# Norms from transposed columns and a transposed inverse in a gated delta rule, a remade normalized input in two feed-forward layers, and an output product in two equal pieces

## The chip, the cores and the metric

The kernel runs on one NeuronCore of a Trainium2 chip. The metric is the device time of one execution in microseconds (us). Five engines work side by side, each on its own queue of instructions: PE (TensorE, the matrix unit; its weight loads are listed apart as PEld), DVE (VectorE), ACT (ScalarE), POOL (GpSimd) and SP (SyncE), which issues the transfers. They wait for each other by semaphores.

## The reference

Two blocks run one behind the other on 512 tokens of width 1024, with 256 context tokens in the first and 16 meta tokens in the second. All in 32 bit:

```python
x   = x   + 0.5*m2  * swiglu(modulate(rmsnorm(x, g1),   m0, m1),  w1_in, w1_out)   # first FFN, 2816 wide
ctx = ctx + 0.5*mc2 * swiglu(modulate(rmsnorm(ctx, g1), mc0, mc1), w1_in, w1_out)
x   = x + m5 * (mix @ w_mix_out)            # attention and a short convolution
x   = x + 0.5*m8 * swiglu(modulate(rmsnorm(x, g2), m6, m7), w2_in, w2_out)          # second FFN
x   = rmsnorm(x, final_norm)
h   = concat(meta, x)                        # 528 tokens
h   = h + hybrid_mixer(rmsnorm(h))           # stick-breaking attention and the gated delta rule
h   = h + swiglu(rmsnorm(h, g3), w3_in, w3_out)                                      # third FFN
```

`modulate(h, shift, scale)` is `h*(1+scale)+shift`, `swiglu` is `(silu(y @ gate) * (y @ up)) @ out`. In the delta rule each of 8 heads has q and k of 128 features, made to unit length per token (`x * rsqrt(sum(x*x) + 1e-6)`), v of 256, and per chunk of tokens a lower triangular matrix `eye + lower`, with `lower` from `k k^T` and a decay, that has to be inverted.

## The kernel before

Activations lie transposed: features on the partitions, tokens in the columns, 8 tiles of 128 features (`self.x[0..7]`). Every large product in 32 bit is made of three fast ones: weights and activations are split into a rounded high part and the rest (`wh`, `wl`, `yh`, `yl`, `hh`, `hl`), and `mm3` (line 204) issues high by high, high by low and low by high for each k of 128 features. A weight tile of 128 by 1024 comes by DMA (`raw`), ACT copies it into `wh` (line 159) and DVE subtracts for `wl` (line 148); `run` loads one job ahead or two, from few buffers. `later` and `tick` put other work behind a certain matmul step of a job, and a scheduler that runs when the kernel is built sets the final order on each engine from the order in the code, the pools' buffers and such marks.

`ffn` (line 285) is used three times: kind A with 512 + 256 columns of tokens (x and the context), kinds B and C with 512. It has 22 hidden tiles f in three groups of 8, 7 and 7. For each f a gate job and an up job multiply by the 8 k of `yh`, `yl`; then 8 out jobs multiply the group's hidden tiles (`hh`, `hl`) into the 8 output tiles and `fin` adds them to x. `yh` and `yl` hold x times a gain, without the norm's factor r per token, which is multiplied on behind the product (`scaled`: DVE, from PSUM). In kind B the shift of `modulate` is carried as two more columns of `yh`, `yl`: the product is cut at 256 columns and has a piece of 258 beside it, and the extra column is the bias of the Silu and an addend of up. In kind C there is no shift, and one piece of 512. In the out jobs of kind A each product has a piece of 512 and one of 256.

The delta rule (`delta`, line 1250) goes head by head, with projections for later heads (`mm3` again, over 264 or 512 columns) put between. `prep` (line 1315) makes the decay, the norms of q and k and the triangular matrix `L`; for the norms ACT squares `kt` (528 columns) and `qt` (512), and PE sums over the partitions with nine fp32 matmuls against one column of ones (lines 1342 to 1344). Later in `prep` four transposes of `kt` and one of its 16 meta columns (lines 1397, 1398) give `kd`, `kdm` by ACT. A solve by 32 on DVE gives `XT`, and `inverse` (line 1430) extends it to 64 and 128: with `X` the transpose of `XT`, it makes `t1 = M XT`, subtracts `X t1` from `XT` (line 1450) and `t1 X` from `X` (line 1451), and repeats with the mask `m6` in place of `m5`.

Of the kernel before, what the change touches and what calls it, by code (L numbers as in the profile page):

```python
# [18 lines left out]
P = 128  # L19
D = 1024  # L20
KD = 8
# [99 lines left out]
class K:  # L121
# [163 lines left out]
    def ffn(self, kind, w_in, w_out, groups, pool, fin, bg=None, early=None):  # L285
        A_, n = kind == "A", (768 if kind == "A" else 512)
        r = self.r
        hid = {}
# [13 lines left out]
        def scaled(ps, nm, more=False):  # L302
            t = pool.tile([P, 770], F32, name=nm, tag=nm, bufs=2)
# [15 lines left out]
        parts = [(0, 0, 512, 512)] + ([(514, 512, 256, 513)] if A_ else [])  # L319

# [29 lines left out]
        def out(grp, f, last):  # L350
            def go(ws):
                ps = self.mmtile()
                pieces = lambda k: [(hid[grp[k]][0][:, o:o + w], hid[grp[k]][1][:, o:o + w]) for _, o, w, _ in parts]
# [14 lines left out]
        self.run(jobs, bg, hold=() if early else (3,))  # L368

# [73 lines left out]
    def ffn1(self):  # L443
        tc, nc = self.tc, self.nc
        with ExitStack() as es:
# [384 lines left out]
    def ffn2(self):  # L830
        tc, nc = self.tc, self.nc
        with ExitStack() as es:
# [6 lines left out]
            self.tt(gm, self.vec("final_norm", 0, 8), self.vec("norm_mix_gain_2", 0, 8), ALU.mult)  # L839

# [9 lines left out]
            self.ffn("B", self.d["w2i"], self.d["w2o"], [list(range(0, 8)), list(range(8, 15)), list(range(15, 22))], pool, fin)  # L850
# [399 lines left out]
    def delta(self, es, eg, gl, kdl, beta, g5, bd, first, free, tail, last):  # L1250
# [8 lines left out]
        def bank(tag="d"):  # L1259
            return qd.tile([P, 512], F32, name=tag, tag=tag, bufs=2)  # L1260
# [54 lines left out]
        def prep(h):  # L1315
# [78 lines left out]

            ps, psm = bank(), bank()
            for c in range(4):
                self.T.transpose(ps[:, c * P:(c + 1) * P], ch(kt, c), idn)
            self.T.transpose(psm[:16, :P], kt[:, :16], idn)
            kd, kdm = tile_("kd", 512, 2), tile_("kdm", P, 2)
            for c in range(4):  # L1400
                self.act(kd[:, c * P:(c + 1) * P], ps[:, c * P:(c + 1) * P], AF.Copy, scale=kdl[:, c, h:h + 1])
            self.act(kdm[:16], psm[:16, :P], AF.Copy, scale=kdl[:16, 4, h:h + 1])
# [27 lines left out]
        def inverse(h):  # L1430
# [242 lines left out]
```

## Time and profile before

| | us |
|---|---|
| three timed runs | 2592.44, 2593.01, 2593.96 |
| median | 2593.01 |
| the profiled execution | 2592.23 |
| its span in the trace | 2590.4 |
| PE busy in the span | 2552.5 (99%) |
| DVE busy | 1683.8 (65%) |
| ACT busy | 1098.0 (42%) |

The span goes from the first to the last instruction of one execution that the hardware profiler recorded; the time of the execution is 1.8 us more. Busy times of one engine's instructions can overlap for PE, which is a pipeline: the mean of one matmul is longer than the distance from its start to the next one's start. How fast PE goes is therefore read from starts. An fp32 matmul that is not split by the kernel appears as two records. The granted clock (PEclk) is 1.00 at 2.4 GHz and 0.50 at 1.2 GHz. Of the stages, the first FFN ends shortly before 620 us, the attention and its convolution lie in 620 to 860, the second FFN in 860 to 1232, stick-breaking attention and the projections around it before 1515, the delta rule in 1515 to 2176, the third FFN from 2225 to the end.

### The profile page before, as it was taken

What the parts mean: (1) busy time and instruction counts of PE and PEld (TensorE: products, weight loads), DVE (VectorE), ACT (ScalarE), POOL (GpSimd) and SP (SyncE); (2) the same over time, 40 slices, a digit from 0 to 9 for tenths busy, and PEclk for the clock granted to TensorE, in tenths of its full rate; (3) what the DMA queues carried; (4) which work ended last, traced back from release to release, by engine and by line L of the source; (5) the groups of instructions that cost most, each with busy time, mean ns of one, the idle gap of its engine ahead of it and who ended that gap; (6) DMA issues with size and microseconds to landing.
All of it is one profiled execution on the core that took longest, in us unless ns stands there. A gap on an engine that the chain in (4) does not pass through costs nothing.

```text
span 2590.4 us, 37782 instructions
## 1 busy us (share of the span) xinstructions
PE 2552.5 (99%) x14983; PEld 2207.9 (85%) x14983; DVE 1683.8 (65%) x3442; ACT 1098.0 (42%) x1898; POOL 15.5 (1%) x11
## 2 busy tenths in 40 slices
PE   7999999999999999999999999999999999999999
PEld 4888888888897999999888888888888877788887
DVE  7865664356879644446777776878888767444443
ACT  7221221235677422224677752554454444422221
POOL 2000000000000000000000000000000000000000
PEclk8999999999999999999999999999999999999999
DMA  7433643222111333333311122222222222333332
GB/s 262 147 115 98 186 142 119 65 59 75 59 33 46 111 91 97 90 98 85 105 58 58 58 89 77 72 59 75 70 64 76 73 80 90 98 92 95 97 98 83
DMA packets 85265, 235.83 MB, mean 91 GB/s; under 512 B 19840, under 2 KB 22592, under 8 KB 85088
## 3 DMA queue, kind: packets, MB, share of 16 engines
q1 hardware_dynamic: 85088, 233.42, 29.5%
q8 instruction: 118, 1.93, 0.3%
q14 instruction: 59, 0.48, 0.1%
HBM read 228.07 MB, written 5.31 MB: 90 GB/s over the span
## 4 chain that ended last, share of the span: by engine, by line
PE 91%; DVE 4%; ACT 2%; DMA 1%; issue 1%; SPq 0%; DVEq 0%; ACTq 0%
PE mm L204 71%; PE mX L204 3%; PE mT L204 3%; DVE wl L148 1%; PE pt L720 1%; PE pt L730 1%; PE e L1505 1%; PE e L1515 1%; PE pv L1147 1%; PE sx L704 1%; PE e L1497 1%; PE e L1498 1%; PE z L204 1%; PE ap L401 1%; PE e L1511 0%
## 5 line engine op out<-in xcount | busy, mean ns | idle before, releaser
L159 ACT ACTIVATE wh<-raw 128x1024 fp32r<-128x1024 f32 (+2 forms) x371 | 375.1, 1013 | 951.1 <-PE mm L204 650.4
L204 PE MATMUL mm<-yh,wh 128*128 128x512 f32 (+2 forms) x2416 | 683.4, 331 | 9.7 <-ACT yh L159 4.9
L204 PE MATMUL mm<-yl,wh 128*128 128x512 f32 (+2 forms) x2416 | 687.4, 333 | 0.0
L204 PE MATMUL mm<-yh,wl 128*128 128x512 f32 (+2 forms) x2416 | 681.1, 331 | 0.0
L204 PEld LDWEIGHTS mm<-yh,wh 128*128 128x128 f32 x2416 | 409.4, 190 | 56.6 <-issue 6.2
L148 DVE TENSOR_TENSOR wl<-raw,wh 128x1024 fp32r<-128x1024 f32 (+2 forms) x371 | 431.1, 1164 | 37.4 <-ACT wh L159 27.1
L204 PEld LDWEIGHTS mm<-yl,wh 128*128 128x128 f32 x2416 | 409.0, 190 | 42.3 <-issue 1.7
L204 PEld LDWEIGHTS mm<-yh,wl 128*128 128x128 f32 x2416 | 409.4, 190 | 41.1 <-issue 1.4
L204 PE MATMUL mm<-hh,wl 128*128 128x512 f32 x704 | 228.1, 364 | 0.0
L204 PE MATMUL mm<-hl,wh 128*128 128x512 f32 x704 | 227.3, 363 | 0.8 <-DVE hl L148 0.8
L204 PE MATMUL mm<-hh,wh 128*128 128x512 f32 x704 | 227.8, 364 | 0.2 <-ACT hh L159 0.2
L148 DVE TENSOR_TENSOR tu<-mm,r 128x512 f32<-128x512 f32 (+1 forms) x66 | 51.4, 779 | 193.7 <-PE mm L204 193.6
L148 DVE TENSOR_TENSOR tg<-mm,r 128x512 f32<-128x512 f32 (+1 forms) x84 | 64.3, 765 | 124.3 <-PE mm L204 124.2
L204 PEld LDWEIGHTS mm<-hl,wh 128*128 128x128 f32 x704 | 120.0, 188 | 23.0 <-DVE hl L148 1.0
L204 PEld LDWEIGHTS mm<-hh,wh 128*128 128x128 f32 x704 | 120.3, 188 | 22.4 <-ACT hh L159 0.5
L204 PEld LDWEIGHTS mm<-hh,wl 128*128 128x128 f32 x704 | 120.0, 188 | 21.0
L151 DVE SCALAR_TENSOR_TENSOR aacc<-araw,csil,aacc 128x1024 f32<-128x1024 f32 x70 | 88.2, 1282 | 60.6 <-DMA araw<-wada 60.6
L151 DVE SCALAR_TENSOR_TENSOR x<-mm,g,x 128x512 f32<-128x512 f32 x48 | 35.8, 747 | 113.1 <-PE mm L204 113.1
L204 PE MATMUL mm<-ych,wh 128*128 128x258 f32 (+1 forms) x368 | 104.3, 283 | 0.0
L204 PE MATMUL mm<-ycl,wh 128*128 128x258 f32 (+1 forms) x368 | 104.1, 283 | 0.0
L204 PE MATMUL mm<-ych,wl 128*128 128x258 f32 (+1 forms) x368 | 103.9, 282 | 0.0
L159 ACT ACTIVATE hh<-tu 128x512 fp32r<-128x512 f32 x88 | 48.5, 575 | 125.6 <-DVE tu L151 106.9
(493 smaller groups left out, 4121.6 us busy)
## 6 DMA issues: line engine op xcount, KB each, us to landing
raw<-win SPq DMA_DIRECT2D x88, 512.0 KB
araw<-wada SPq DMA_DIRECT2D x60, 512.0 KB
raw<-w1i SPq DMA_DIRECT2D x44, 512.0 KB
raw<-w2i SPq DMA_DIRECT2D x44, 512.0 KB
raw<-w3i SPq DMA_DIRECT2D x44, 512.0 KB
raw<-wmi SPq DMA_DIRECT2D x18, 512.0 KB
raw<-wbd SPq DMA_DIRECT2D x16, 512.0 KB
raw<-w1o SPq DMA_DIRECT2D x16, 448.0 KB
```

The lines of the kernel that those rows point to most:

```text
L148: return self.V.tensor_tensor(out=out, in0=a, in1=b, op=op)
L151: return self.V.scalar_tensor_tensor(out=out, in0=a, scalar=s, in1=b, op0=op0, op1=op1)
L159: return self.A.activation(out=out, in_=a, func=func, bias=bias, scale=scale, **kw)
L204: last = self.T.matmul(o, lhsT=w[a], rhs=yy[b], start=start and i == 0, stop=stop and i == 2)
L401: self.T.matmul(ps[h][:4], lhsT=self.csr4[:, k, :], rhs=w, start=k == 0 and i == 0, stop=k == KD - 1 and i == 1)
L704: self.T.matmul(sx[:, :512], lhsT=lq, rhs=kk[:, :512], start=i == 0, stop=i == 1)
L720: self.T.transpose(ps[:, (2 * kt + qt) * P:(2 * kt + qt + 1) * P], pr[qt][:, (2 * c + kt) * P:(2 * c + kt + 1) * P], self.cs("ident"))
L730: self.T.matmul(ps[:, :256], lhsT=vs[:, kt, g, :], rhs=pp[kt // 2][i][:, (kt % 2) * 256:(kt % 2 + 1) * 256], start=kt == 0 and i == 0, sto ...
L1147: self.T.matmul(pv[:, c0:], lhsT=a[:m, j], rhs=b, start=j == 4 and i == 0, stop=i == 2, skip_group_check=True)
L1497: self.T.matmul(ps[:, :256], lhsT=ch(kt, c), rhs=S0, start=True, stop=True)
L1498: self.T.matmul(ps[:, 256:], lhsT=ch(qt, c, 0), rhs=S0, start=True, stop=True)
L1505: self.T.matmul(ps[:, :256], lhsT=ch(XT, c, 0), rhs=vi, start=True, stop=True)
```

## The change

There are four parts.

First, the out product of kind A is cut into 384 + 384 columns. They lie in columns 128 to 896 of the PSUM tile, so that each half stays in one bank, and `fin` reads x from 128:640 and the context from 640:896.

Second, kinds B and C make a full y while the first jobs run: `remake` forms for each k `z = x * r * gain (+ shift)` on DVE, splits it into `zh` (ACT) and `zl` (DVE), two k in each of the jobs 2 to 5 (counted from 0). From job 8 on, the gate and up jobs multiply by z (`gate2`, `up2`) in one piece of 512 columns, Silu reads PSUM, and no r, no bias and no extra columns are left there. The small `pad` tiles move the addresses.

Third, `prep` transposes `kt` (4 + 1, formerly further on) and `qt` (4, new) and takes the norms by ACT, Square with a sum along the row, one for each 128 tokens; the copies into `kd` and `kdm` stand between them. The nine matmuls against ones are gone.

Fourth, `inverse` no longer makes `t1 X`; the second step's `X` is the transpose of the new `XT`, by four PE transposes and an ACT copy, and the mask `m6` is applied earlier.

```diff
@@ ffn
         def scaled(ps, nm, more=False):
-            t = pool.tile([P, 770], F32, name=nm, tag=nm, bufs=2)
+            t = pool.tile([P, wide], F32, name=nm, tag=nm, bufs=2)
...
+        halves = [(0, 128, 384), (384, 512, 384)] if A_ else [(0, 0, 512)]
+
+        def gate2(f):
+            def go(ws):
+                ps = self.mmtile()
+                self.gemm([ps[:, :512]], ws, KD, remade[1])
+                t = pool.tile([P, wide], F32, name="tg", tag="tg", bufs=2)
+                self.last_silu = self.act(t[:, :512], ps[:, :512], AF.Silu)
+                gu[f] = t
+            return go
+
+        def up2(f, slot):
+            def go(ws):
+                ps = self.mmtile()
+                self.gemm([ps[:, :512]], ws, KD, remade[1])
+                t = pool.tile([P, wide], F32, name="tu", tag="tu", bufs=2)[:, :512]
...
+                self.tt(t, ps[:, :512], gu.pop(f)[:, :512], ALU.mult)
+                self.split(hh, hl, t)
+                hid[f] = (hh, hl)
+            return go
@@ out
-                self.gemm([ps[:, o:o + w] for _, o, w, _ in parts], ws, len(grp), pieces)
+                self.gemm([ps[:, c:c + w] for _, c, w in halves], ws, len(grp), pieces)
@@
-                jobs.append(([(w_in[f], 1024)], gate(f)))
-                jobs.append(([(w_in[NF + f], 1024)], up(f, i)))
+                new = remade and len(jobs) >= remade[0]
+                jobs.append(([(w_in[f], 1024)], (gate2 if new else gate)(f)))
+                jobs.append(([(w_in[NF + f], 1024)], (up2 if new else up)(f, i)))
@@
+    def remake(self, pool, gain, shift):
+
+        hi = [pool.tile([P, S], F32R, name=f"zh{k}", tag=f"zh{k}") for k in range(KD)]
+        lo = [pool.tile([P, S], F32R, name=f"zl{k}", tag=f"zl{k}") for k in range(KD)]
+
+        def one(k):
+            t = pool.tile([P, S], F32, name="zt", tag="zt", bufs=2)
+            self.tt(t, self.x[k], self.r[:, :S], ALU.mult)
+            if shift is None:
+                self.make_y(k, t, gain(k), hi[k], lo[k])
+            else:
+                self.ts(t, t, gain(k), ALU.mult, shift(k), ALU.add)
+                self.split(hi[k], lo[k], t)
+
+        def step(i):
+            if 0 < i <= KD // 2:
+                for k in (2 * i - 2, 2 * i - 1):
+                    self.later(4 * (k % 2) + 1, lambda k=k: one(k))
+        return step, lambda k: [(hi[k], lo[k])]
@@ ffn1, fin
-                self.stt(self.x[f], ps[:, :512], g2[:, 0, f:f + 1], self.x[f], ALU.mult, ALU.add)
-                self.stt(self.ctx[f], ps[:, 512:768], g2[:, 1, f:f + 1], self.ctx[f], ALU.mult, ALU.add)
+                self.stt(self.x[f], ps[:, 128:640], g2[:, 0, f:f + 1], self.x[f], ALU.mult, ALU.add)
+                self.stt(self.ctx[f], ps[:, 640:896], g2[:, 1, f:f + 1], self.ctx[f], ALU.mult, ALU.add)
@@ ffn2
+            g7 = pool.tile([P, 8], F32, name="g7")
+            self.stt(g7, self.mx[:, 7, :], 1.0, self.vec("norm_ffn2", 0, 8), ALU.add, ALU.mult)
+            pad = pool.tile([P, 24], F32, name="pad")
+            nc.vector.memset(pad[:, :1], 0.0)
+            step, y = self.remake(pool, lambda k: g7[:, k:k + 1], lambda k: self.mx[:, 6, k:k + 1])
...
+                     bg=step, remade=(7, y))
@@ delta, prep
-            u = tile_("cu", T, 2)
-            self.act(u, kt, AF.Square)
-            u2 = tile_("cu", T, 2)
-            self.act(u2[:, :S], qt, AF.Square)
-            ps = bank()
-            one = cs("ones", 1)
-            for c in range(4):
-                self.T.matmul(ps[:, c:c + 1], lhsT=ch(u, c), rhs=one, start=True, stop=True)
-                self.T.matmul(ps[:, 5 + c:6 + c], lhsT=ch(u2, c, 0), rhs=one, start=True, stop=True)
-            self.T.matmul(ps[:16, 4:5], lhsT=u[:, :16], rhs=one, start=True, stop=True)
...
-            self.ts(nk[:, 0:4], ps[:, 0:4], EPS, ALU.add)
-            self.ts(nk[:, 5:9], ps[:, 5:9], EPS, ALU.add)
-            self.ts(nk[:16, 4:5], ps[:16, 4:5], EPS, ALU.add)
...
+            ps, psm = bank(), bank()
+            for c in range(4):
+                self.T.transpose(ps[:, c * P:(c + 1) * P], ch(kt, c), idn)
+            self.T.transpose(psm[:16, :P], kt[:, :16], idn)
+            for c in range(4):
+                self.act(u[:, :P], ps[:, c * P:(c + 1) * P], AF.Square, accum_out=nk[:, c:c + 1])
+                self.act(kd[:, c * P:(c + 1) * P], ps[:, c * P:(c + 1) * P], AF.Copy, scale=kdl[:, c, h:h + 1])
+            self.act(u[:16, :P], psm[:16, :P], AF.Square, accum_out=nk[:16, 4:5])
+            self.act(kdm[:16], psm[:16, :P], AF.Copy, scale=kdl[:16, 4, h:h + 1])
+            ps = bank()
+            for c in range(4):
+                self.T.transpose(ps[:, c * P:(c + 1) * P], ch(qt, c, 0), idn)
+            for c in range(4):
+                self.act(u[:, :P], ps[:, c * P:(c + 1) * P], AF.Square, accum_out=nk[:, 5 + c:6 + c])
+            self.ts(nk, nk, EPS, ALU.add)
@@ delta, inverse
-            ps, ps2 = bank(), bank()
-            for c in range(4):
-                self.T.matmul(c_(ps, c), lhsT=c_(X, c), rhs=c_(t1, c), start=True, stop=True)
-                self.T.matmul(c_(ps2, c), lhsT=c_(t1, c), rhs=c_(X, c), start=True, stop=True)
-            self.tt(XT, XT, ps, ALU.subtract)
-            self.tt(X, X, ps2, ALU.subtract)
-            self.tt(m3(M), m3(L), bc(cs("m6")), ALU.mult)
...
+            self.tt(m3(M), m3(L), bc(cs("m6")), ALU.mult)
+            self.tt(XT, XT, ps, ALU.subtract)
+            yield
             ps, ps2 = bank(), bank()
...
             self.act(t1, ps, AF.Copy)
+            for c in range(4):
+                self.T.transpose(c_(ps2, c), c_(XT, c), idn)
+            self.act(X, ps2, AF.Copy)
@@ ffn3
-            pad = pool.tile([P, 144], F32, name="pad")
+            pad = pool.tile([P, 48], F32, name="pad")
+            nc.vector.memset(pad[:, :1], 0.0)
+            step, y = self.remake(pool, lambda k: self.vec("norm_ffn_gain_2", k), None)
+            pad = pool.tile([P, 32], F32, name="pad2")
...
+                     bg=step, remade=(7, y))
```

What the scheduler makes of it on the engines, at three places. First PE in the delta rule, where a head's norms are made; `cst` is the tile of constants (the ones, or the unit matrix of a transpose), `cu` the squares. Before:

```order
L204 MATMUL mm<-yh_78,wl 128x264 x2
L1342 MATMUL d<-cst,cu 128x1
L1364 MATMUL d<-kt 128x128 x4
L204 MATMUL mm<-yh_79,wh 128x264 x2
...
L204 MATMUL mm<-yl_88,wh 128x264
L1343 MATMUL d<-cst,cu 128x1
L1342 MATMUL d<-cst,cu 128x1
...
L1344 MATMUL d<-cst,cu 16x1
L204 MATMUL mm<-yl_88,wh 128x264
```

And after the change, in the same head:

```order
L204 MATMUL mm<-yl_84,wh 128x264
L1393 MATMUL d<-cst,kt 128x128 x4
L1394 MATMUL d<-cst,kt 16x128
L204 MATMUL mm<-yl_84,wh 128x264
...
L204 MATMUL mm<-yl_81,wh 128x264 x2
L204 MATMUL mm<-yh_73,wl 128x264 x2
L1402 MATMUL d<-cst,qt 128x128 x4
L1420 MATMUL d<-kt 128x128 x3
L1584 MATMUL e<-cst,o 128x128 x2
```

The block of one-column matmuls is gone; the transposes of `kt` stand earlier among the projection's matmuls, those of `qt` some ten products later, ahead of `k k^T`.

Second, PE in a head's `inverse`, from the first correction to the last product. Before:

```order
L1450 MATMUL d<-t_18639,x_71 128x128
L1451 MATMUL d<-x_71,t_18639 128x128
...
L204 MATMUL mm<-yh_79,wh 128x512
L1458 MATMUL d<-XT,x_70 128x128 x4
L204 MATMUL mm<-yl_87,wh 128x512
L204 MATMUL mm<-yh_79,wl 128x512
L204 MATMUL mm<-yh_80,wh 128x512
L204 MATMUL mm<-yl_88,wh 128x512
L1462 MATMUL d<-t_18639,x_71 128x128 x4
```

And after, where line 1506 is the new transpose and `x_71` is X:

```order
L1497 MATMUL d<-t_17757,x_71 128x128 x4
L204 MATMUL mm<-ogh_17435,wl 128x512
L204 MATMUL mm<-ogh_17445,wh 128x512
L1533 MATMUL e<-vbm,XTm 16x256
L1503 MATMUL d<-XT,x_70 128x128 x4
L1506 MATMUL d<-cst,XT 128x128 x4
L1537 MATMUL e<-vn,kdm 128x256
L204 MATMUL mm<-ogl_17446,wh 128x512
L204 MATMUL mm<-ogh_17445,wl 128x512
L1510 MATMUL d<-t_17757,x_71 128x128 x4
```

Between the product into t1 (1458, now 1503) and the last one (1462, now 1510) stand four transposes and three other matmuls in place of four other matmuls.

Third, DVE in the second FFN, jobs 2 and 3, with the new operations on `zt` and `zl` among the evictions `tg`, `tu` and the weight differences `wl`:

```order
L148 TENSOR_TENSOR wl<-raw,wh 128x1024
L148 TENSOR_TENSOR zt<-x_64,r 128x512
L151 SCALAR_TENSOR_TENSOR tu<-tu,tg 128x512
L156 TENSOR_SCALAR zt<-zt,g_7894,mx 128x512
L148 TENSOR_TENSOR zt<-x_65,r 128x512
L148 TENSOR_TENSOR hl<-tu,hh 128x512
L148 TENSOR_TENSOR zl_7906<-zt,zh_7898 128x512
L156 TENSOR_SCALAR zt<-zt,g_7894,mx 128x512
L148 TENSOR_TENSOR wl<-raw,wh 128x1024
L148 TENSOR_TENSOR tg<-mm,r 128x512
```

Before, the same stretch from `wl` to `tg` has `wl` a second time, `tu`, a small reduction and `hl`, and nothing of z.

## Rows read from the trace of the kernel before

**Rows 1.** The page, busy time, share of the span, instructions of each engine.

```profile
PE 2552.5 (99%) x14983; PEld 2207.9 (85%) x14983; DVE 1683.8 (65%) x3442; ACT 1098.0 (42%) x1898; POOL 15.5 (1%) x11
```

**Rows 2.** Windows by stage: length, busy PE, PEld, DVE, ACT, POOL, PEclk, DMA, GB/s.

```profile
620.00:860.00 240.00, 232.10 (x1581) 207.36 (x1580) 206.41 (x401) 173.87 (x308) 0.00 (x0) 1.00 0.18 54
860.00:1232.00 372.00, 370.19 (x2625) 348.81 (x2623) 183.25 (x268) 120.42 (x154) 0.00 (x0) 1.00 0.32 95
1515.00:2176.00 661.00, 657.50 (x3911) 558.82 (x3912) 512.60 (x1410) 294.90 (x548) 0.00 (x0) 0.99 0.25 73
2225.00:2590.40 365.40, 361.67 (x1570) 294.34 (x1568) 153.43 (x180) 97.30 (x114) 0.00 (x0) 1.00 0.31 94
```

**Rows 3.** Waits (us, times, longest): whole run, then 1515 to 2176.

```profile
PE mm L204 <- ACT wh L159: 0.9, 1, 0.9
ACT wh L159 <- PE mm L204: 128.3, 53, 7.2
```

**Rows 4.** Timeline of PE (start, duration): where jobs begin in the three FFNs.

```profile
187.18 0.51 PE L204 MATMUL mm<-hh,wh 128*128 128x512 f32 x2
...
254.85 0.47 PE L204 MATMUL mm<-yh,wh 128*128 128x512 f32 x1
...
1113.11 0.40 PE L204 MATMUL mm<-yh,wh 128*128 128x256 f32 x2
...
1193.19 0.40 PE L204 MATMUL mm<-hh,wh 128*128 128x512 f32 x1
...
2432.41 0.40 PE L204 MATMUL mm<-hh,wh 128*128 128x512 f32 x1
...
2470.53 0.40 PE L204 MATMUL mm<-yh,wh 128*128 128x512 f32 x1
...
2548.39 0.40 PE L204 MATMUL mm<-hh,wh 128*128 128x512 f32 x1
```

**Rows 5.** Groups by form (busy, mean ns, idle before); then a window of six jobs.

```profile
L148 DVE TENSOR_TENSOR tu<-mm,r 128x512 f32<-128x512 f32 x44 | 30.4, 692 | 145.1 <-PE mm L204 145.1
...
L159 ACT ACTIVATE vb<-e,co 128x128 f32<-128x128 f32 x64 | 18.2, 367 | 10.7 <-PE e L1474 10.5
...
L159 ACT ACTIVATE t<-d 128x512 f32<-128x512 f32 x16 | 9.6, 597 | 16.2 <-PE d L1458 14.1 <-PE d L1445 2.1
...
871.20:905.50 34.30, 34.29 (x288) 34.30 (x289) 17.07 (x26) 11.46 (x14) 0.00 (x0) 1.00 0.36 108
```

**Rows 6.** Timeline of PE in the delta rule: one-column matmuls, transposes, inverse.

```profile
1629.91 0.36 PE L1343 MATMUL d<-cst,cu 128*128 128x1 f32 x2
...
1631.55 0.20 PE L1344 MATMUL d<-cst,cu 128*16 128x1 f32 x2
1631.68 0.50 PE L204 MATMUL mm<-yl,wh 128*128 128x512 f32 x1
...
1669.95 0.65 PE L1474 MATMUL e<-cst,vt 128*128 128x128 f32 x4
1670.44 0.27 PE L1475 MATMUL e<-cst,vt 128*16 128x128 f32 x1
...
1759.10 0.39 PE L1451 MATMUL d<-x,t 128*128 128x128 f32 x2
1759.32 0.39 PE L1450 MATMUL d<-t,x 128*128 128x128 f32 x2
```

**Rows 7.** Windows in the delta rule, columns as in Rows 2.

```profile
1537.64:1541.05 3.41, 3.41 (x18) 3.41 (x17) 3.41 (x9) 0.90 (x2) 0.00 (x0) 0.50 0.21 46
1541.05:1544.46 3.41, 3.41 (x31) 3.39 (x30) 2.95 (x17) 0.69 (x2) 0.00 (x0) 1.00 0.28 108
...
1633.22:1636.63 3.41, 3.41 (x9) 2.64 (x9) 2.68 (x17) 0.00 (x0) 0.00 (x0) 0.50 0.08 25
...
2018.92:2022.33 3.41, 3.41 (x17) 3.41 (x17) 1.68 (x5) 0.35 (x1) 0.00 (x0) 0.50 0.00 0
```

**Rows 8.** PE's groups by form in 620 to 860.

```profile
L720 PE MATMUL pt<-cst,pp 128*128 128x128 f32 x192 | 31.7, 276 | 2.5 <-ACT pp L159 1.8 <-DVE ptl L148 0.7
```

More of the change, by code (lines that the diff above doesn't have):

```diff
@@ L282, in make_y, with ffn @@
         self.stt(dl, src, gain, dh.bitcast(F32), ALU.mult, ALU.subtract)
-    def ffn(self, kind, w_in, w_out, groups, pool, fin, bg=None, early=None):
+    def ffn(self, kind, w_in, w_out, groups, pool, fin, bg=None, early=None, remade=None):
         A_, n = kind == "A", (768 if kind == "A" else 512)
         r = self.r
+        wide = 770 if A_ else 544
         hid = {}
@@ L319, in ffn @@
         parts = [(0, 0, 512, 512)] + ([(514, 512, 256, 513)] if A_ else [])
+        halves = [(0, 128, 384), (384, 512, 384)] if A_ else [(0, 0, 512)]
[12 more added lines that the diff above has]
+                t = pool.tile([P, wide], F32, name="tu", tag="tu", bufs=2)[:, :512]
+                hh = pool.tile([P, n], F32R, name="hh", tag=f"hh{slot}")
+                hl = pool.tile([P, n], F32R, name="hl", tag=f"hl{slot}")
+                self.tt(t, ps[:, :512], gu.pop(f)[:, :512], ALU.mult)
+                self.split(hh, hl, t)
+                hid[f] = (hh, hl)
+            return go
         def gate(f):
@@ L352, in go @@
                 ps = self.mmtile()
-                pieces = lambda k: [(hid[grp[k]][0][:, o:o + w], hid[grp[k]][1][:, o:o + w]) for _, o, w, _ in parts]
-                self.gemm([ps[:, o:o + w] for _, o, w, _ in parts], ws, len(grp), pieces)
+                pieces = lambda k: [(hid[grp[k]][0][:, o:o + w], hid[grp[k]][1][:, o:o + w]) for o, _, w in halves]
+                self.gemm([ps[:, c:c + w] for _, c, w in halves], ws, len(grp), pieces)
                 fin(f, ps, last)
@@ L848, in fin @@
                     self.sq_add(f, self.x[f], 512, 1024, pool, scale=self.vec("final_norm", f))
-            self.ffn("B", self.d["w2i"], self.d["w2o"], [list(range(0, 8)), list(range(8, 15)), list(range(15, 22))], pool, fin)
+            self.ffn("B", self.d["w2i"], self.d["w2o"], [list(range(0, 8)), list(range(8, 15)), list(range(15, 22))], pool, fin,
+                     bg=step, remade=(7, y))
             ms = pool.tile([P, KD, NM], F32, name="msq")
@@ L1333, in prep @@
             yield
[L1335 to L1344 removed]
             nk, rr = tile_("nk", 9, 2), tile_("rr", 9, 2)
             nc.vector.memset(nk, 1.0)
[L1347 to L1349 removed]
+            kd, kdm = tile_("kd", 512, 2), tile_("kdm", P, 2)
+            u = tile_("cu", T, 2)
+            ps, psm = bank(), bank()
[13 more added lines that the diff above has]
+            self.ts(nk, nk, EPS, ALU.add)
             self.rsqrt_small(rr, nk, tile_("na", 9, 2), tile_("nb", 9, 2))
@@ L1393, in prep @@
             self.tt(at, ps, at, ALU.mult)
-            ps, psm = bank(), bank()
-            for c in range(4):
[L1397 to L1402, printed above, removed]
             s.update(at=at, kd=kd, kdm=kdm, L=L)
@@ L1447, in inverse @@
             yield
-            ps, ps2 = bank(), bank()
+            ps = bank()
             for c in range(4):
                 self.T.matmul(c_(ps, c), lhsT=c_(X, c), rhs=c_(t1, c), start=True, stop=True)
-                self.T.matmul(c_(ps2, c), lhsT=c_(t1, c), rhs=c_(X, c), start=True, stop=True)
+            self.tt(m3(M), m3(L), bc(cs("m6")), ALU.mult)
             self.tt(XT, XT, ps, ALU.subtract)
-            self.tt(X, X, ps2, ALU.subtract)
-            self.tt(m3(M), m3(L), bc(cs("m6")), ALU.mult)
             yield
-            ps = bank()
+            ps, ps2 = bank(), bank()
             for c in range(4):
@@ L1614, in fin @@
                     nc.sync.dma_start(self.d["out"][f], self.x[f])
-            self.ffn("C", self.d["w3i"], self.d["w3o"], [list(range(0, 8)), list(range(8, 15)), list(range(15, 22))], pool, fin)
+            self.ffn("C", self.d["w3i"], self.d["w3o"], [list(range(0, 8)), list(range(8, 15)), list(range(15, 22))], pool, fin,
+                     bg=step, remade=(7, y))
     def body(self, upto=9):
```

## The prediction

> **What bounds the kernel now.** I read the busy times first: PE works for 2552.5 of 2590.4 us, DVE for 65% and ACT for 42% of the span [rows 1]. An average can hide a stage with another limit, so the table by stage came next: in the second FFN (860 to 1232), the delta stage (1515 to 2176) and the third FFN with what leads into it (2225 to the end) PE is busy for 370 of 372, 657.5 of 661 and 361.7 of 365.4 us [rows 2]. A busy PE need not be at its peak, since matmuls are pipelined; what must be seen is who waits for whom. PE waited once in the whole run for split weights, for 0.9 us, while ACT's weight split waited 53 times in the delta stage alone, 128.3 us, until PE gave a buffer back [rows 3]. So the time is a sum of matmul paces, and an edit is worth what it does to the spacing of starts on PE, not to the "busy" of one matmul. Only the granted clock stands beside that: 1.00 in three of the stages, 0.99 in delta [rows 2].
>
> The sum is made against the profiled execution, 2592.2 us, of which 2590.4 are the span; the median of the three timed runs is 2593.0, 0.8 above it, and I add that at the end.
>
> **Second FFN.** A gate or up job is 8 k of three products, 24 in all, each in two pieces, 256 and 258 columns. Of such jobs 14 lie between the starts 1113.11 and 1193.19, so one takes 80.08/14 = 5.72 us, 238 ns a product [rows 4]. Of the 44 jobs, counted from 0, those from 8 on (36) have one 512-wide matmul in place of the two pieces. What does one cost? The rows have two answers. The out-products (moving operand `hh`) between 2432.41 and 2470.53 are 168 (8 jobs of 7 k, three each): 38.12/168 = 226.9 ns. The third FFN's gate and up jobs (operand `yh`) are 14 between 2470.53 and 2548.39: 77.86/14 = 5.561 us a job, 231.7 ns a product [rows 4]. Same columns, same clock, other tile. The new operands `zh` and `zl` are tiles of their own, 512 wide, padded so that their addresses fall as those of `hh` and `hl` do (64 bytes past a multiple of 256; `yh` and `yl` have 2112-byte rows and drift), so I take 226.9: 24 of them are 5.446 us, and 36 × (5.720 − 5.446) = **−9.9 us**. With `yh`'s 231.7 it is 36 × (5.720 − 5.561) = −5.7, the other bound.
>
> Making z costs DVE three 512-wide operations a k and ACT one copy, for 8 k in jobs 2 to 5. The nearest row for a DVE pass is 692 ns [rows 5], so 24 passes are 16.6 us. In the six jobs from 871.2 to 905.5 DVE is busy for 17.1 of 34.3 us [rows 5]; 33.7 fit, barely, and the first reader of z is job 8, two jobs after the last pass. The cover is the weight split, two jobs ahead; if an eviction or a `wl` lies behind z all the same, PE stands for the 2 or 3 us by which the four jobs overflow (22.9 us of time for about 11.4 + 16.6 of work), less the head start. I take 0 and keep +4 as a bound. What leaves (r-multiply, 2-column copies) was DVE work under PE: nothing.
>
> **Third FFN.** The matmuls keep their 512 columns and only change tiles: 36 × (5.561 − 5.446) = **−4.1 us**, from 0 (if the address is not the cause) to −4.1. Its z needs two DVE passes a k: covered.
>
> **First FFN's out-product.** 512+256 becomes 384+384, the same columns. Between 187.18 and 254.85 lie 192 pairs (8 jobs of 8 k, three each) at 352.4 ns [rows 4]. A 384 has no row. By the line through the shorter and the full piece (238.3/2 = 119 ns at some 257 columns, 226.9 to 231.7 at 512) one takes 173 to 175 ns, a pair 346 to 351. There are 22 × 8 × 3 = 528 pairs: −3.4 to −0.9; should a split at 384 bring nothing and lose a little, +2. I take **−1.5**.
>
> **Norms in the delta rule.** Out go nine fp32 matmuls of one column a head. The row at 1629.91 begins such a run: seven of them until 1631.55, 0.23 each, then the one on 16 rows until 1631.68, 0.13 [rows 6]. One column costs as much as a product of 128 columns there (0.22 us from 1759.10 to 1759.32 [rows 6]). Between those two a full one is 0.224: a head is 8 × 0.224 + 0.13 = 1.92 us, eight heads 15.4. In come four transposes of q a head; those of k were there, and move ahead. Four transposes take 0.49 us from 1669.95 to 1670.44, 0.12 each [rows 6]: 32 × 0.12 = 3.9. Together **−11.5**.
>
> ACT takes nine Square operations of 128 columns for two wide ones. An ACT operation of 128 columns fills 18.2/64 = 0.28 us, a 512-wide one 0.60 [rows 5]: nine for two is 9 × 0.28 − 2 × 0.60 = 1.3 us more a head. The run, 14 operations with the five `kd` copies that were there before, 4 to 5 us, stands ahead of a weight split `wh` on ACT. ACT's reserve is the waiting of [rows 3], 128.3/53 = 2.4 us each time, more than the 1.3 that is new: 0 expected.
>
> **Transposed inverse.** Out: four fp32 products a head, 0.22 each, 32 × 0.22 = 7.0. In: four transposes, 32 × 0.12 = 3.9. Together **−3.2**. The change adds a wait: X now comes by a 512-wide ACT copy (597 ns [rows 5]) that is queued behind the copy of t1, and the last product needs both. Before, four 512-wide matmuls (0.9 us) stood between to cover t1's copy; now the transposes (0.5) and about three other products (0.7) cover two copies, 1.2 us of work and the hops between. I take 0.3 a head, **+2.4**; bounds 0 and 1.2 × 8 = +10. DVE loses a pass of some 0.7 us a head, off the path.
>
> **The clock.** In three stretches of 3.41 us the granted clock is 0.50 (1.2 of 2.4 GHz): from 1537.64, 1633.22 and 2018.92 [rows 7]. Each begins about 2 us behind a run of one-column matmuls (that at 1629.91 to 1631.68 is the one of [rows 6]); such a stretch holds 18, 9 and 17 matmuls, the one behind the first 31 [rows 7]. Half of 3.41 is 1.7 lost, 18 of 31 matmuls say 1.4: 1.5 each, **−4.5** if the dips go with the matmuls. Transposes as such do not bring them: 192 lie in 620 to 860 [rows 8], where the clock is 1.00 [rows 2]. Bounds 0 and −5.1.
>
> The Trainium skill, "TensorE: Matmul & The Clock Gate", Part 4, says that a PE transpose does not count as busy for the full clock in the way of a matmul. By that rule the dips would stay, and the sum would be 4.5 us smaller; the stretch just named disagrees, though no row has transposes right behind the delta stage's matmuls in the new number.
>
> **Sum.** −9.9 − 4.1 − 1.5 − 11.5 − 3.2 + 2.4 − 4.5 = −32.3; 2592.2 − 32.3 + 0.8 = 2560.7, said as **2560 us**.
>
> **Rivals.** *The columns decide, not the tile*: z is read at `yh`'s pace, the FFNs give −5.7 and 0, the sum −24.0: 2569. For it: I have one pair of paces and other differences than the address lie between them. Against: the operand is all that differs on PE. The same skill page ("Back-to-back issue gap") gives columns/2.4 plus 2.5 ns per matmul. By it the second FFN gains 36 × 24 × 3.4 ns = 2.9 us and the third nothing; 226.9 against 231.7 ns for the same 512 columns disagrees.
>
> *The dips stay*, as transposes and short products take the places of the one-column matmuls: −27.8, 2565.
>
> *The inverse's new wait is open*: +10 instead of +2.4, with the evictions of PSUM behind it: −24.7, 2568.
>
> *ACT becomes the bound of delta, and it ends slower.* The norm run of 14 operations stands in one queue with `wh`. If the two copies and nine squares hold a weight split up beyond its reserve, PE stands in every head. It decides from 32.3/8 = 4.0 us a head on. With a run twice its price, some 10 us, less the 2.4 us of reserve, 8 × 7.6 = 61 us are lost: 2622; with 5 lost a head, 2601 (more than 2593). Against: ACT is busy for 295 of 661 us there [rows 2], and PE never waited for more than 0.9.
>
> **How the numbers follow.** Forecast 0.62; columns decide 0.13; dips stay 0.08; inverse wait 0.11; ACT bounds it 0.04; the rest (0.02) a change that does nothing, were the removed PE time given back elsewhere. The low end takes the good bounds together (−3.4 in the first FFN, −5.1 for the clock, 0 for the inverse): −37.2, and a few us for what a lighter DVE gives: 2550. The high end holds two of the mild rivals at once: −32.3 + 8.3 + 7.6 = −16.4, 2576, taken as 2575. Within 0.2%, about what a measurement of this kernel can tell from no change, means within 5 us: faster 0.93, same 0.03, slower 0.04.
>
> **What would show it.** Second-FFN jobs from the ninth on at 5.45 us a job (5.56: the columns decide); the same in the third; out-product pairs of the first FFN at 346 to 351 ns; no one-column block and no stretch at 0.50 in delta, which ends some 17 us shorter; DVE dense in jobs 2 to 7 with PE unbroken. Wrong would make it: PE waiting for `wh`, `bd` or the X copy by more than 0.5 us a head, or z's passes holding up an eviction.

## The result

The changed kernel takes 2561.11 us (median of four runs, 2559.76 to 2563.32), the kernel before 2593.49 in the same comparison: a ratio of 0.9874, 95% interval 0.9857 to 0.9891. That is 32.4 us less; 32.3 were worked out and 2560 was forecast. The profiled execution of the changed kernel is the longest of its four, 2563.32 us, with a span of 2561.5.

### The profile after

The page's busy times of the changed kernel, and then four windows (columns as in Rows 2): the delta rule, two stretches at half the clock, and 860 to 1232 with the second FFN. The delta rule and the third FFN begin 7 and 26 us earlier now.

```profile
PE 2521.7 (98%) x13975; PEld 2171.1 (85%) x13975; DVE 1652.0 (64%) x3353; ACT 1115.9 (44%) x2052; POOL 15.6 (1%) x11
```

```profile
1508.00:2150.00 642.00, 638.30 (x3766) 540.50 (x3767) 509.20 (x1386) 310.42 (x685) 0.00 (x0) 1.00 0.25 75
383.44:386.85 3.41, 3.41 (x11) 3.33 (x11) 1.59 (x4) 0.95 (x1) 0.00 (x0) 0.50 0.30 118
803.28:806.69 3.41, 3.15 (x9) 2.57 (x9) 3.33 (x7) 2.50 (x5) 0.00 (x0) 0.50 0.00 0
860.00:1232.00 372.00, 369.81 (x1829) 313.89 (x1828) 176.42 (x244) 127.36 (x177) 0.00 (x0) 1.00 0.32 97
```

PE still fills the stages, with 1008 instructions fewer. The delta rule's clock is 1.00 where it was 0.99 [rows 2]; none of the three stretches at 0.50 of [rows 7] ("dips" below) has an answer there. But two dips have come up elsewhere: one at 383.44, in the first FFN's out product, which the change cuts differently, and one at 803.28, in the attention block, which the change does not touch.

The paces come from starts on PE, as in [rows 4]; here are the first FFN's out product, and the edges of 14 jobs in the second and in the third FFN:

```profile
188.40 0.51 PE L204 MATMUL mm<-hh,wh 128*128 128x384 f32 x2
...
254.94 0.51 PE L204 MATMUL mm<-hh,wl 128*128 128x384 f32 x2
...
1110.04 0.39 PE L204 MATMUL mm<-zh,wh 128*128 128x512 f32 x1
...
1186.20 0.39 PE L204 MATMUL mm<-hh,wh 128*128 128x512 f32 x1
...
2443.39 0.39 PE L204 MATMUL mm<-zh,wh 128*128 128x512 f32 x1
...
2519.55 0.39 PE L204 MATMUL mm<-hh,wh 128*128 128x512 f32 x1
```

A job with z takes 76.16/14 = 5.440 us in both FFNs, 226.7 ns a product; 5.446 was the term. The 191 pairs between 188.40 and 254.94 stand 66.54/191 = 348.4 ns apart; 346 to 351 was the bound. From the end of the second FFN to the last product of the delta rule's stage the trace of before goes from 1231.06 to 2173.16, that of after from 1224.05 to 2147.40: 942.1 became 923.4, 18.8 less, where 16.8 were worked out.

### The profile page after: what moved, and what is told of

Its sections match the earlier page's. It is cut to its first block, busy times and chain, and to the rows that moved or that the text cites. A ratio compares the mean times of both kernels' runs of the same rounds, so it can differ in the third digit from the quotient of the medians.

```text
span 2561.5 us, 35787 instructions
## 1 busy us (share of the span) xinstructions
PE 2521.7 (98%) x13975; PEld 2171.1 (85%) x13975; DVE 1652.0 (64%) x3353; ACT 1115.9 (44%) x2052; POOL 15.6 (1%) x11
## 4 chain that ended last, share of the span: by engine, by line
PE 91%; DVE 4%; ACT 3%; issue 1%; DMA 1%; DVEq 0%; ACTq 0%
PE mm L204 71%; PE mX L204 3%; PE mT L204 3%; PE pt L766 1%; PE pt L776 1%; PE e L1553 1%; DVE wl L148 1%; PE e L1563 1%; PE pv L1199 1%; PE sx L750 1%; PE e L1545 1%; PE e L1546 1%; PE z L204 1%; DMA araw<-wada 1%; PE e L1559 1%
## 5 line engine op out<-in xcount | busy, mean ns | idle before, releaser
L204 PE MATMUL mm<-yh,wh 128*128 128x512 f32 (+3 forms) x1552 | 455.9, 339 | 10.3 <-ACT yh L159 4.3
L204 PE MATMUL mm<-yl,wh 128*128 128x512 f32 (+3 forms) x1552 | 454.9, 338 | 0.0
L204 PE MATMUL mm<-yh,wl 128*128 128x512 f32 (+3 forms) x1552 | 451.5, 336 | 0.0
L204 PEld LDWEIGHTS mm<-yh,wl 128*128 128x128 f32 x1552 | 264.6, 189 | 29.2 <-issue 1.0
L204 PE MATMUL mm<-hl,wh 128*128 128x384 f32 (+1 forms) x704 | 227.4, 364 | 0.7 <-DVE hl L148 0.7
L204 PE MATMUL mm<-hh,wh 128*128 128x384 f32 (+1 forms) x704 | 227.3, 363 | 0.8 <-ACT hh L159 0.8
L204 PE MATMUL mm<-hh,wl 128*128 128x384 f32 (+1 forms) x704 | 227.8, 364 | 0.0
L204 PE MATMUL mm<-zh,wh 128*128 128x512 f32 x576 | 224.1, 389 | 0.0
L204 PE MATMUL mm<-zl,wh 128*128 128x512 f32 x576 | 224.1, 389 | 0.0
L204 PE MATMUL mm<-zh,wl 128*128 128x512 f32 x576 | 224.1, 389 | 0.0
```

The lines of the kernel that those rows point to most:

```text
L204: last = self.T.matmul(o, lhsT=w[a], rhs=yy[b], start=start and i == 0, stop=stop and i == 2)
```

## The experiments

### Each part alone

Four kernels: the kernel before with one part of the change. Between them they are the whole diff.

```diff
# halves_alone: in out() of ffn, and the two slices of fin in ffn1
...
-                self.gemm([ps[:, o:o + w] for _, o, w, _ in parts], ws, len(grp), pieces)
+                self.gemm([ps[:, c:c + w] for _, c, w in halves], ws, len(grp), pieces)
...
# remade_alone: gate2, up2, remake, bg=step, remade=(7, y)
# norms_alone: the new prep      # inverse_alone: the new inverse
```

> The kernel before with the first FFN's out product in 384 + 384 columns and nothing else. Theory of the prediction: pairs start 346 to 351 ns apart in place of 352.4, 528 pairs, -0.9 to -3.4 us in the out blocks, so 2590 to 2592 us, which a timing cannot tell from no change. Rival (a piece's fixed cost decides and two pieces cost the same however they are cut): pairs stay at 352, 0 us. The delta rule is untouched here: if the stretches of granted clock 0.50 there belong to the one-column matmuls, this profile shows two to four of them right behind such blocks; if they come by chance, they lie elsewhere.

> The kernel before with the remade y in the second and third FFN and nothing else. Theory of the prediction (the tile's address sets 226.9 ns a product): jobs of 5.45 us in both, -9.9 - 4.1 = -14.0, 2579 us. Rival (columns decide): 5.56 us a job, -5.7 and 0, 2587 us. Second rival (z's passes on DVE stop PE): a gain smaller by up to 4 us, seen as idle PE in jobs 2 to 8. Delta is untouched: the stretches at 0.50 come again behind the one-column blocks, if those bring them.

> The kernel before with the norms by transposes and ScalarE and nothing else. Theory of the prediction: -11.5 us of PE and -4.5 for the clock, 2577 us, and no stretch at 0.50 in the delta rule. Rival (the stretches stay, or come elsewhere): -11.5, 2581.5. Rival (ACT holds the weights up): less than -8 and PE waiting for wh.

> The kernel before with the transposed inverse and nothing else. Theory of the prediction: 3.2 us of PE less, 2.4 us of new wait for X, -0.8, 2592 us, not to be told from no change by time; the trace shows PE waiting for X some 0.3 us a head ahead of the last product. Rival (wait open): +4 to +7, 2597 to 2600, with 0.8 to 1.2 us a head. Rival (wait wholly covered): -3.2, 2590.

The kernel before has 2592.17 us here (21 runs).

| part alone | worked out | median us | difference | ratio, 95% interval |
|---|---|---|---|---|
| 384 + 384 | -1.5 | 2590.52 | -1.7 | 0.9993, 0.9985 to 1.0002 |
| remade y | -14.0 | 2578.73 | -13.4 | 0.9949, 0.9937 to 0.9961 |
| norms | -16.0 | 2576.92 | -15.3 | 0.9942, 0.9930 to 0.9955 |
| inverse | -0.8 | 2589.72 | -2.5 | 0.9991, 0.9982 to 1.0000 |

The four differences add up to -32.8, the whole to -32.4: within the noise of these medians, some 2 us, the parts neither help nor hinder each other. The first and the last cannot be told from no change by time. For the halves the trace speaks:

```profile
188.42 0.34 PE L204 MATMUL mm<-hh,wh 128*128 128x384 f32 x1
...
254.96 0.51 PE L204 MATMUL mm<-hh,wl 128*128 128x384 f32 x2
```

That is 66.54 us for 191 pairs, 348.4 ns as in the whole change, against 352.4 [rows 4]. The rival that cutting elsewhere brings nothing falls, for 528 × 4 ns = 2 us. This profile gives the gain back in a dip at 383.58, though, of which more below.

For the inverse, the view of one line: what PE waited for ahead of the last product, first line 1462 of the kernel before, then line 1463 of inverse_alone and line 1510 of the changed kernel (us, times):

```profile
  ACT t L159: 2.1, 8
```

```profile
  ACT x L159: 2.5, 7
```

```profile
  ACT x L159: 2.1, 6
```

The wait for X is there, 2.5 and 2.1 us in seven and six heads, much as the 2.4 of the prediction. But it adds little or nothing: before, PE waited 2.1 us in eight heads for t1 at the same place, which the prediction had taken for covered by four products. So of the term +2.4 at most 0.4 is left, and the part is worth about its PE time: -2.5 by the medians, whose interval reaches to 0, for the -3.2 that was worked out. In the delta rule the missing 2.4 would account for the 2 us by which the stage gained more than was said.

### What sets the pace of a product

The forecast rested on z lying as hh does. This was tried by moving z alone, then the weights alone, then everything.

```diff
# z_at_128 (second FFN; in the third in the same way)
-            pad = pool.tile([P, 24], F32, name="pad")
+            pad = pool.tile([P, 40], F32, name="pad")
...
+            pad = pool.tile([P, 48], F32, name="pad2")
# weights_at_128: raw, wh, wl 64 bytes on, the rest of 256 behind them
             self.r = perm.tile([P, 2 + S + C], F32, name="r")
+            pad = perm.tile([P, 16], F32, name="pad")
...
+            pad = self.perm.tile([P, 48], F32, name="pad3")
# all_at_128: only the first of the two
```

> The changed kernel with 64 bytes of padding more ahead of zh and zl and the rest of 256 behind them, so that z lies 128 bytes past a multiple of 256 while hh, hl stay at 64. Theory (the address of the moving operand sets the pace): z's products go from 226.9 back to about 232 ns, 72 jobs of 24, 72 x 24 x 5 ns = +8.6 us against the changed kernel, about 2570 us, with the out jobs unchanged. Rival (that z is a tile of its own, without r or extra columns behind it, sets the pace): no change, 2561 us.

> The changed kernel with wh and wl (and raw) moved by 64 bytes, to 128 past a multiple of 256; z and hh stay at 64. Theory A (64 is good as such for the moving operand): products of z and hh stay at 227 ns, 2561 us. Theory B (the moving operand is fast where it lies as the weights do): z and hh go to 232, 5 ns x some 2800 products of 512 columns, +14 us, 2575 us, and the yh at 128 get faster.

> The changed kernel with raw, wh, wl and all that lies behind them on the left moved by 64 bytes, so that the weights and z, hh lie at 128 together. Theory (the moving operand is fast where it lies as the weights do, modulo 256): z and hh at 226 to 228 ns a product again, out blocks 43.3 and 37.9 us long as in the changed kernel, 2560 to 2562 us. Rival (64 is good for weights or operand as such): 230 to 233 ns, out blocks of 44.6 and 39.0, 2570 to 2577.

| kernel | weights at (mod 256) | z at | hh at | ns a product: z | hh | median us |
|---|---|---|---|---|---|---|
| changed | 64 | 64 | 64 | 226.7 | 226.7 | 2561.11 |
| z_at_128 | 64 | 128 | 64 | 233.3, then 228.9; mean 229.9 | 226.9 | 2567.11 |
| weights_at_128 | 128 | 64 | 64 | 233.3 | 233.3 | 2577.31 |
| all_at_128 | 128 | 128 | 128 | 226.7 | 226.7 | 2562.18 |

The addresses are those that the kernels give their tiles; a trace does not show them. The ns are means of the starts' distances by operand. The rows behind them, in the second FFN: of z_at_128 the edges of the first eight z jobs, then of the last 14,

```profile
906.91 0.40 PE L204 MATMUL mm<-zh,wh 128*128 128x512 f32 x1
...
951.71 0.40 PE L204 MATMUL mm<-hh,wh 128*128 128x512 f32 x1
...
1110.32 0.40 PE L204 MATMUL mm<-zh,wh 128*128 128x512 f32 x1
...
1187.25 0.40 PE L204 MATMUL mm<-hh,wh 128*128 128x512 f32 x1
```

of weights_at_128 the 14 jobs and the end of the out products behind them,

```profile
1111.85 0.39 PE L204 MATMUL mm<-zh,wh 128*128 128x512 f32 x1
...
1190.25 0.39 PE L204 MATMUL mm<-hh,wh 128*128 128x512 f32 x1
...
1229.22 0.40 PE L204 MATMUL mm<-hh,wl 128*128 128x512 f32 x1
```

and of all_at_128:

```profile
1106.05 0.39 PE L204 MATMUL mm<-zh,wh 128*128 128x512 f32 x1
...
1182.21 0.39 PE L204 MATMUL mm<-hh,wh 128*128 128x512 f32 x1
...
1220.06 0.39 PE L204 MATMUL mm<-hh,wl 128*128 128x512 f32 x1
```

The 14 jobs take 76.93, 78.40 and 76.16 us, against 76.16 in the changed kernel; the out products behind them take 38.97 us in weights_at_128 and 37.85 in all_at_128. Same instructions, same order, same clock of 1.00: only addresses differ. The rival that a tile of its own makes z fast falls with the first kernel, and the absolute address falls with the third: 128 is as good as 64 when both operands lie there. At these two places the products are fastest where the moving operand lies as the weights do, modulo 256 bytes. Moving the weights alone cost 16 us in a kernel of 2561.

The yh, yl of the third FFN, whose rows of 2112 bytes step by 64 modulo 256 from one k to the next, bear this out. In the changed kernel k = 3 and 7 are the fastest, 230.0 and 230.2 ns, the others 231.9 to 232.9; with the weights 64 bytes on they are k = 0 and 4, 230.2 and 230.0, the others 231.6 to 233.2. Their mean over k hardly moved (231.8 and 232.0): that the yh at 128 get faster came for those k, while k = 3 and 7 lost as much.

The remainder is not all of it. In z_at_128 the first eight z jobs of either FFN, which follow jobs with y, take 44.80/8 = 5.600 us (233.3 ns a product), and the other 28, which follow out products, 5.495 (228.9 ns), from the same tiles. Why stays open. So the 6.0 us that this kernel costs are less than the 8.6 expected.

### What lowered the clock in the delta rule

Two kernels: the kernel before with the nine matmuls against 128 columns of ones, and the changed kernel with nine one-column matmuls a head put back.

```diff
# ones_128wide
-            one = cs("ones", 1)
+            one = cs("ones")
...
-                self.T.matmul(ps[:, c:c + 1], lhsT=ch(u, c), rhs=one, start=True, stop=True)
+                self.T.matmul(ps[:, c * P:(c + 1) * P], lhsT=ch(u, c), rhs=one, start=True, stop=True)
...
# ones_back, in prep of the changed kernel
...
+            for c in range(4):
+                self.T.matmul(ps[:, c:c + 1], lhsT=ch(kt, c), rhs=one, start=True, stop=True)
+                self.T.matmul(ps[:, 5 + c:6 + c], lhsT=ch(qt, c, 0), rhs=one, start=True, stop=True)
+            self.T.matmul(ps[:16, 4:5], lhsT=kt[:, :16], rhs=one, start=True, stop=True)
+            self.V.tensor_copy(tile_("dead", 9, 2)[:, :4], ps[:, 0:4])
```

> The kernel before, with its nine fp32 matmuls for the norms made 128 columns wide (against 128 columns of ones in place of one; the norms are read from one of the equal columns). Theory (the dips belong to matmuls that have one column): the matmuls cost the same 0.22 us, no stretch at 0.50 in the delta rule, 2 to 3 dips of 1.5 us gone: 2588 to 2590. Rival (any block of such fp32 matmuls lowers the clock, however wide): two or three dips in delta as before, 2592. Rival (a one-column matmul is cheaper than the rows show): each costs more, 2592 to 2600.

> The changed kernel, with nine fp32 matmuls of one column a head added again in the delta rule (k and q themselves against the ones), whose sums nothing of the result uses. Theory: 15.4 us of PE, as the price was worked out, and up to three stretches at 0.50 of 1.5 us behind such blocks: +15 to +20, 2576 to 2581 us, with a granted clock of 0.993 to 0.994. Rival (the matmuls fit into PE's gaps and the norms gained by shorter waits): +5 to +10, 2566 to 2571. Rival (no lower clock without the squares on ACT ahead): +15, and no stretch at 0.50 in delta.

The wide ones: 2591.52 us (10 runs) against 2592.09, ratio 0.9996 (0.9987 to 1.0006). The block on PE and the window of the stage:

```profile
1628.64 1.05 PE L1343 MATMUL d<-cst,cu 128*128 128x128 f32 x8
1629.62 0.39 PE L1345 MATMUL d<-cst,cu 128*16 128x128 f32 x2
1629.95 0.50 PE L204 MATMUL mm<-yh,wh 128*128 128x512 f32 x1
```

```profile
1515.00:2176.00 661.00, 656.11 (x3914) 556.04 (x3913) 518.41 (x1411) 302.20 (x553) 0.00 (x0) 1.00 0.25 73
```

A block with 128 times the columns takes hardly longer: eight records in 0.98 us, 0.24 for a matmul of two records, where one column had 0.22 to 0.23. Only the one on 16 rows is dearer, 0.33 in place of 0.13. The clock of the stage is 1.00 and has no stretch at 0.50; the mean granted clock of all ten timed runs is 0.995 to 0.996, where the kernel before has 0.992 to 0.995 in the same comparison. The time hardly moved all the same: at the prediction's 1.5 us a dip the three of before were worth 4.5 us, but the eight matmuls of a head cost some 0.02 us more each (1.3 in all), the 16-row ones 1.6 in all, and PE's waits for `bd` went from 1.7 to 2.1 us. That leaves an estimate of 1.2 us; the stage is 1.4 us shorter in the profile (942.1 and 940.7). The median alone would prove nothing.

Put back into the changed kernel, they bring both costs: 2578.69 us (2574.57 to 2582.39), +17.6 against the changed kernel, of which 15.4 had been worked out as PE time. In the profile the stretch from the second FFN's end to the last product of the delta rule's stage is 20.3 us longer (943.7 and 923.4), with three dips: 15.4 + 3 × 1.5 = 19.9. Its windows, and the first block:

```profile
1530.06:1533.47 3.41, 3.41 (x17) 3.41 (x17) 3.33 (x6) 0.72 (x4) 0.00 (x0) 0.50 0.01 2
1625.63:1629.04 3.41, 3.41 (x13) 2.33 (x12) 3.02 (x21) 0.00 (x0) 0.00 (x0) 0.50 0.54 154
1656.35:1659.76 3.41, 3.41 (x18) 3.40 (x18) 3.19 (x9) 1.04 (x7) 0.00 (x0) 0.50 0.03 5
```

```profile
1528.03 0.34 PE L1408 MATMUL d<-cst,kt 128*128 128x1 f32 x2
...
1529.87 0.20 PE L1410 MATMUL d<-cst,kt 128*16 128x1 f32 x2
```

Three dips again, each 1.9 to 3.2 us behind the start of a one-column block. Both rivals fall with them: that the matmuls fit into PE's gaps, and that the dips need the squares on ACT ahead. Counted over all traces: in the five kernels with such blocks (before, halves, remade y, inverse, ones_back) 12 of 40 heads have a dip, which begins 1.9 to 6.7 us behind the head's first one-column matmul and no more than 1.9 us behind the start of its last; in the nine without them 72 heads have none. The runs' spread follows it: the four of ones_back have 2574.57 us at a clock of 0.996 and 2582.39 at 0.993.

A shorter block is not enough. The stick-breaking attention has blocks of five such matmuls, about 1.0 us long where the nine take 1.9, eight in each of the 14 traces, and no dip follows any of them; the first of before:

```profile
1251.82 1.08 PE L1032 MATMUL z<-cst,pu 128*128 128x1 f32 x10
```

### Gains that the kernel leaves, and a wait that it adds

The trace after shows one new wait. PE and ACT at the start of the third FFN, in the changed kernel:

```profile
2208.62 0.51 PE L204 MATMUL mm<-yh,wh 128*128 128x512 f32 x1 [1.18 <-DVE tg L148]
```

```profile
2200.84 1.28 ACT L159 ACT_TABLE_LOAD   x1 [3.39 <-DVE rv L156]
2202.14 0.63 ACT L159 ACTIVATE ra<-rv 128x512 f32<-128x512 f32 x1
```

and ACT at that place before:

```profile
2223.24 1.28 ACT L159 ACT_TABLE_LOAD   x1
2226.57 0.63 ACT L159 ACTIVATE ra<-rv 128x512 f32<-128x512 f32 x1 [2.05 <-DVE rv L156]
```

Before, ACT loaded its table for the logarithm while DVE still made `rv`; now the load stands behind the wait for `rv`, and 1.28 us come between. The remade y brings it: alone, it shows the same 3.39 us ahead of the load and 1.14 us of PE waiting. The reason is a reading of the two kernels that no run shows by itself: the first operation now has two waits, one for DVE and one for ACT's own earlier work (with the new tiles, `ra` lies elsewhere), and the one for DVE has been put on the load ahead of it. r comes late, the eviction `tg` comes late, and PE stands 1.18 us.

Three kernels build on the changed one: the left-hand tiles of the second mixer at 64, then also the remade y from job 6 on, then also the table load placed by hand.

```diff
# og_at_64
             g5 = b2.tile([P, 5, 8], F32, name="g5")
+            pad = b2.tile([P, 40], F32, name="pad")
# best: og_at_64 and
-                     bg=step, remade=(7, y))
+                     bg=step, remade=(5, y))
# best2: best and
...
-            self.r_from_acc(self.r, [(0, 0, 512)], pool, ...)
+            pre = self.pin(self.last_sq)
+            with tc.issue_after(pre.ins):
+                self.r_from_acc(self.r, [(0, 0, 512)], pool, ...)
```

> The changed kernel with 160 bytes of padding at the end of the second mixer's left pool, so that oh, ol, ogh, ogl and mgh move from 160 to 64 past a multiple of 256. Theory (address): their 512-wide products go from some 232.5 to 227 ns, about 700 of them, -3.9 us, 2557 us. Rival (only FFN tiles behave so): no change, 2561.

> The changed kernel with oh, ol, ogh, ogl and mgh at 64 (as in og_at_64) and the remade y used from job 6 on in place of 8. Expected by the paces seen: two jobs of 0.27 us less in the second FFN and two of 0.1 in the third, -0.7 against og_at_64: 2558 us, between 2555 and 2560. Rival (z's last passes are late for job 6 and PE waits for them): 1 to 3 us lost again, 2559 to 2562.

> The kernel best (operands at 64, remade y from job 6), with the ACT table for Ln and Exp loaded right behind the last Square ahead of the third FFN. In the changed kernel that load waits for rv (3.4 us idle, then 1.28), before the change it did not, and PE stands 1.18 us behind it. Theory: PE's wait for tg at the third FFN's start goes, -1.2 us against best, 2557.7 us, between 2555 and 2559, below the spread of single runs, so the trace decides. Rival (the wait for tg has another cause): PE still waits 1.2 us there.

| kernel | median us | ratio to before, 95% interval |
|---|---|---|
| changed | 2561.11 | 0.9874, 0.9857 to 0.9891 |
| og_at_64 | 2558.93 | 0.9873, 0.9859 to 0.9887 |
| best | 2558.95 | 0.9868, 0.9853 to 0.9882 |
| best2 | 2556.05 | 0.9855, 0.9837 to 0.9872 |

og_at_64: the products with `oh` and `ol` go from means of 231.5 and 237.0 ns to 227.3 and 226.5, but those with `ogh`, mixed with smaller matmuls, only from 234.7 to 231.3, and the stretch from the second FFN's end to the third's first out product is 1.8 us shorter, not 3.9. The direction is that of the theory, the size was half of it. The step to best is too small for these runs. In best2, ACT at the same place:

```profile
2191.34 1.28 ACT L258 ACT_TABLE_LOAD   x1
2194.73 0.63 ACT L159 ACTIVATE ra<-rv 128x512 f32<-128x512 f32 x1 [2.10 <-DVE rv L156]
```

The load is done before `rv` arrives, the second load (for Exp) has gone, and PE waits for nothing there. The intervals of the four overlap, so best2's further 5 us rest on the medians and on these rows.

## Why the prediction was right

**What bounds it.** It named PE's spacing as the sum to make. With the parts measured alone, each came within 1.7 us of its terms, and they added up. That the whole came within 0.1 us of -32.3 is luck in part: the inverse gave 1.7 us more than was said, the remade y and the norms 0.6 and 0.7 less. One reading was wrong without harm: PE waited for split weights not once in the whole run, but also at line 401, within the first 55 us and far from the change:

```profile
PE ap L401 <- ACT wh L159: 6.3, 1, 6.3
```

**Second and third FFN.** 5.446 us a job was taken from the out products by their address; 5.440 came. The choice between the two paces that [rows 4] offered was the largest one in the text (8.3 us between the ends), and its ground, the address, holds in the runs, though in another form: not 64 as such, but the same remainder as the weights. The rival by columns falls. The formula of the Trainium skill ("TensorE: Matmul & The Clock Gate", "Back-to-back issue gap"), which the page gives for a single matmul's gap, comes to an estimate of 215.8 ns for 512 columns and has no term for the address; 226.7 to 233.3 were measured for the same 512, so here the measurement decides.

z's passes on DVE were said to fit barely, 33.7 of 34.3 us. The window of the same six jobs after the change shows 32.2, and 1.35 us of PE idle at its start:

```profile
872.40:906.70 34.30, 32.95 (x277) 32.78 (x276) 32.23 (x63) 18.64 (x29) 0.00 (x0) 1.00 0.31 94
```

```profile
874.35 0.47 PE L204 MATMUL mm<-yh,wh 128*128 128x256 f32 x2 [1.35 <-DVE tg L316]
```

That idle time is the first eviction's, 1.26 us before the change too; behind it PE runs through. Nothing for z, as taken. The term missed the 1.2 us of the table load in the third FFN, a step that the working does not have, and that may be the 1.0 us between the jobs' gain and the part's: the jobs alone give 36 × (5.720 − 5.440) + 36 × (5.561 − 5.440) = 14.4, and the part alone is worth 13.4.

**First FFN.** 348.4 ns lies in the interpolated 346 to 351: 528 × 4.0 = 2.1, for 1.5 taken. In the profiled execution the first FFN ends 1.7 us later than before all the same, 1.2 of it because its first out product starts later (187.18 and 188.40), and in the rest lies the dip at 383.44. From the first out product to the last the five kernels with 512 + 256 take 424.7 to 426.0 us and the six with 384 + 384 and no dip 422.0 to 424.1; the changed kernel, halves_alone and ones_back, with 384 + 384 and a dip at 383, take 425.8 to 426.2. So the split gains its 2 us, and such a dip takes them back. PE stood twice just ahead of it, for the group's last hidden tile:

```profile
381.72 0.75 PE L204 MATMUL mm<-hh,wh 128*128 128x384 f32 x2 [0.77 <-ACT hh L159]
383.19 1.02 PE L204 MATMUL mm<-hl,wh 128*128 128x384 f32 x2 [0.71 <-DVE hl L148]
```

These waits are there before the change too (0.21 and 0.77 us). The prediction has no term for the dip; three of nine kernels with the split show it and none of the five without, too few to tell whether the split brings it.

**Norms.** −11.5 for PE and −4.5 for the clock; −15.3 measured, and in the profile of norms_alone the delta rule's stretch is 15.9 us shorter (942.1 and 926.2). The transposes fell under the price of the rows (four of q in 0.41 to 0.49 us, for 0.49), and ACT kept up: PE's products in this stage waited for `wh` once, 0.9 us, as before [rows 3]. The clock's share was not measured alone; the 19.9 against 20.3 of ones_back bear it out. The rule that transposes do not count as work for the full clock (the Trainium skill, same page, Part 4) would have left the dips; the 64 heads with more transposes and no dip, in eight kernels, speak against it for this stage.

**Inverse.** The one term whose working failed: +2.4 for a wait as though there had been none before. PE's waiting at line 1462 was in the trace, and it was 2.1 us. It should have been subtracted. Of the rivals written for the part alone, the one by which the new wait is wholly covered (2590) fits the 2589.72 us, but by another way: the wait is there and replaces an old one.

**The rivals** of ACT as the bound and of an open wait did not come. The dips of the delta rule did not stay; of the two others in the profile of the changed kernel, the one at 803.28 lies where the change does nothing, the one at 383.44 in the out product.

## What to carry to other kernels

A stage that PE fills is costed by distances between starts, and a distance has to be taken from rows with the same addresses as the new operand will have: here 2 to 7 ns in 227 on 1728 products of z were worth 6.0 us, more than two of the four parts. Where a new wait is priced, look up first what the engine already waits for at that instruction. And after a change of tiles, look at the waits of the first instruction behind each table load.

## What the runs showed of the hardware that had not been expected

A 512-column product of this kind takes 226.7 ns where the moving operand and the weights have the same remainder modulo 256 bytes, and 228.9 to 233.3 where they differ by 64 (four kernels above); `ogh` at 160 shows 234.7 and at 64 231.3 among other work. What sets the pace between 228.9 and 233.3 at the same addresses was not tried.

An fp32 matmul on 128 rows against one column costs what one against 128 columns does (0.22 to 0.24 us), and of the blocks of nine such matmuls 12 of 40 were followed by 3.41 us at half the clock; the same blocks at 128 columns were not in the eight heads of their profile, and the mean clock of their ten timed runs (0.995 to 0.996) agrees. Why only some of the blocks are followed by a dip stays open.

The attention block shows dips of its own in some executions, at 690 to 693 and at 799 to 804 us, in the traces of the changed kernel, norms_alone, z_at_128, weights_at_128 and all_at_128 and in none of the other nine, with the same instructions there. The one at 803.28 follows 1.80 us in which PE waited for `pp`, but best has the same 1.80 us wait at this place and no dip. What decides it was not tried.
